# ScalarE's first two DMAs in a top-2 expert combine change places

## Chip, cores and metric

The kernel runs on one core of one Trainium2 chip. The metric is the device time of one execution in microseconds (us), taken as the median of several runs. A program page of the profile describes one execution of it. Engines are named as there: DVE is VectorE, ACT is ScalarE, SP is SyncE (it only issues transfers here), POOL is GpSimd. A name with a q behind it (ACTq, SPq) is the part of an engine that issues DMAs and waits.

## Reference

Each of 16 x 1024 tokens has two expert outputs of 512 numbers and two weights. The result is the weighted sum of the two.

```python
def setup_inputs():
    batch, seq, hidden, n_experts, k = 16, 1024, 512, 8, 2
    # expert_outputs (batch, seq, k, hidden), combine_weights (batch, seq, k), float32
def reference(expert_outputs, combine_weights):
    weights = combine_weights[..., np.newaxis]
    return np.sum(expert_outputs * weights, axis=2).astype(np.float32)
```

So 67 MB are read, 34 MB are written, and there are two multiplications and one addition for each number of the output.

## The kernel before, in words

The 16384 tokens are spread over 128 partitions, 128 tokens to each: the first 115 of a partition's tokens are neighbours in memory, and so are its last 13. A partition's share is worked through in ten tiles of 13, 13, 12, 13, 13, 13, 12, 13, 13 and 13 tokens. SBUF has room for four tiles (the array `et`); tile g lies in room g modulo 4, and the result of a tile overwrites the front half of a room, from where it is stored.

**Tiles 0 to 7** take two DVE instructions each: a multiplication of the whole tile by its weights, in place (L98), and an addition of the two halves (L99). Tile 8 is shared between ACT (L91) and DVE (L93, L95, L99). Tile 9 is done token by token, ACT multiplying one half (L74) and DVE doing the rest (L75).

**Transfers.** SP issues the loads (L68). Tile 0 is loaded in two pieces: two tokens in rows cut to 4 KB (called load 0a here, 256 rows of 4 KB) and the other eleven (load 0b, 128 rows of 45 KB). Loads 1, 2 and 3 follow, 128 rows of 48 or 52 KB each. Load 4 and the later ones each wait until the result that used their room has been stored. The stores of tiles 0 to 6 are issued by ACT (L121), the last two by SP: one for tiles 7 and 8 together, and one for tile 9.

**Around the change.** The order of instructions is written by hand; on each engine they stand in the order of the code. DVE's first instruction (L102) fills a small tile `zt` (16 partitions x 128 numbers) with zeros. ACT's first three instructions are DMAs: `zt` to 16 places of the output, 512 bytes each (L105); the main weights, 230 numbers for each partition, which serve tiles 0 to 8 (L71, called by the first `weights(...)`); and the last tile's weights, 26 numbers for each partition (L71, the second call). The zeros are overwritten later by the store of the results; the first store waits for them. Then comes a small ACT instruction that has the activation table loaded (L108). DVE's first multiplication (L98 of tile 0) waits for load 0a, load 0b and the main weights.

The queue of SP's DMAs is q1 in the profile, that of ACT's is q10. Each DMA over 128 partitions gives each of 16 DMA engines eight data packets (load 0a sixteen) and one packet of 4 bytes that signals the end; the zeros give each engine one data packet and one signal.

Of the kernel before, what the change touches and what calls it, by code (L numbers as in the profile page):

```python
# [1 line left out]

# [4 lines left out]


@with_exitstack
def kernel(  # L10
    ctx: ExitStack,
    tc: tile.TileContext,
    expert_outputs: bass.AP,
    combine_weights: bass.AP,
    out: bass.AP,
):

    nc = tc.nc
    b, s, k, h = expert_outputs.shape
    assert k == 2
    n = b * s
    P = nc.NUM_PARTITIONS
    per = n // P
    assert per * P == n

    SIZES = [13, 13, 12, 13]
    ROOMS = len(SIZES)  # L30
    ROOM0 = [sum(SIZES[:r]) for r in range(ROOMS)]
    TILES = [13, 13, 12, 13, 13, 13, 12, 13, 13, 13]
    FIRST = [2, 11, 13, 12, 13]
    STORES = [[0], [1], [2], [3], [4], [5], [6], [7, 8], [9]]
    MIXED = {8: 3}
    LAST = 115
    N = len(TILES)
    assert sum(TILES) == per
    starts = [sum(TILES[:g]) for g in range(N)]

    def rows(x):

        first = x[0 : P * LAST, :].rearrange("(p t) f -> p t f", p=P)
        second = x[P * LAST : n, :].rearrange("(p t) f -> p t f", p=P)
        return lambda t, c: first[:, t : t + c, :] if t < LAST else second[:, t - LAST : t - LAST + c, :]

    flat = out.rearrange("b s h -> (b s) h")
    eo = rows(expert_outputs.rearrange("b s k h -> (b s) (k h)"))
    cw = rows(combine_weights.rearrange("b s k -> (b s) k"))
    o = rows(flat)  # L50

    dt = mybir.dt.float32
    mult = mybir.AluOpType.mult
    add = mybir.AluOpType.add
    copy = mybir.ActivationFunctionType.Copy

    pool = ctx.enter_context(tc.tile_pool(name="all", bufs=1))
    et = pool.tile([P, sum(SIZES), k * h], dt)
    halves = et.rearrange("p j (k h) -> p (j k) h", k=k)
    wt = pool.tile([P, per * k], dt)  # L60
    wk = wt.rearrange("p (t k) -> p t k", k=k)
    zt = pool.tile([16, 128], dt)
    warm = pool.tile([P, 1], dt)

    def load(g, skip=0, c=None, **kw):
        c = TILES[g] - skip if c is None else c
        at = ROOM0[g % ROOMS] + skip
        nc.sync.dma_start(out=et[:, at : at + c], in_=eo(starts[g] + skip, c), **kw)  # L68

    def weights(q, t, c):  # L70
        q.dma_start(out=wk[:, t : t + c, :], in_=cw(t, c))  # L71

    def pair(t, x0, x1, y):
        nc.scalar.activation(out=x0, in_=x0, func=copy, scale=wt[:, k * t : k * t + 1])  # L74
        nc.vector.scalar_tensor_tensor(  # L75
            out=y, in0=x1, scalar=wt[:, k * t + 1 : k * t + 2], in1=x0, op0=mult, op1=add
        )

    def combine(g, base):
        at, c, t0 = ROOM0[g % ROOMS], TILES[g], starts[g]  # L80
        room = halves[:, k * at : k * (at + c), :]
        x0, x1 = et[:, at : at + c, 0:h], et[:, at : at + c, h : 2 * h]
        if g == N - 1:
            for i in range(c):
                pair(t0 + i, x0[:, i, :], x1[:, i, :], halves[:, base + i, :])
            return
        if g in MIXED:
            v = MIXED[g]
            for i in range(v, c):
                x = x0[:, i, :]  # L90
                nc.scalar.activation(out=x, in_=x, func=copy, scale=wt[:, k * (t0 + i) : k * (t0 + i) + 1])  # L91
            w0 = wk[:, t0 : t0 + v, 0:1].to_broadcast([P, v, h])
            nc.vector.tensor_tensor(out=x0[:, 0:v, :], in0=x0[:, 0:v, :], in1=w0, op=mult)  # L93
            w1 = wk[:, t0 : t0 + c, 1:2].to_broadcast([P, c, h])
            nc.vector.tensor_tensor(out=x1, in0=x1, in1=w1, op=mult)  # L95
        else:
            wb = wt[:, k * t0 : k * (t0 + c)].unsqueeze(2).to_broadcast([P, k * c, h])
            nc.vector.tensor_tensor(out=room, in0=room, in1=wb, op=mult)  # L98
        nc.vector.tensor_tensor(out=halves[:, base : base + c, :], in0=x0, in1=x1, op=add)  # L99

    with tc.manual_schedule():
        nc.vector.memset(zt, 0.0)  # L102

        ahead = flat[0 : P * LAST, :].rearrange("(q t) h -> q (t h)", q=16)
        nc.scalar.dma_start(out=ahead[:, 0:128], in_=zt)  # L105
        weights(nc.scalar, 0, LAST)
        weights(nc.scalar, LAST, per - LAST)
        nc.scalar.activation(out=warm, in_=nc.const_aps.tensor(1.0, (P, 1), dt), func=copy)  # L108

        load(0, 0, 2, max_dma_last_dim=k * h * 4)  # L110
        load(0, 2)
        for g in range(1, ROOMS):
            load(g)
        for j, st in enumerate(STORES):
            base = k * ROOM0[st[0] % ROOMS if st != [N - 1] else (N - 4) % ROOMS]
            c = 0
            for g in st:
                combine(g, base + c)
                c += TILES[g]
            q = nc.sync if j in (7, 8) else nc.scalar  # L120
            q.dma_start(out=o(starts[st[0]], c), in_=halves[:, base : base + c, :])  # L121
            for g in st:
                if g + ROOMS < N:
                    load(g + ROOMS)


# [1 line left out]
_INS = ['expert_outputs', 'combine_weights']  # L128
_OUTS = [((16, 1024, 512), 'float32')]


# [23 lines left out]
```

## Time and profile before

| what | value |
|---|---|
| median of 3 runs | 238.88 us (238.88 to 238.91) |
| the profiled execution's own time | 238.91 us |
| its span, first to last record | 237.1 us |
| DVE busy | 190.0 us |
| ACT busy | 15.8 us |
| HBM traffic | 100.80 MB, 425 GB/s over the span |

The profiled execution is the slowest of the three runs' range, 0.03 us above the median. Its time is 1.8 us longer than its span. The span's start is the zero of all times in the views. A line such as `1.43 18.04 DMA wt<-in_combine_weights_dram` in the chain reads: from 1.43 us on, for 18.04 us, the chain was a transfer into `wt`. A row of the list of issues ends with KB for each and the median time from issue to landing. A row of a DMA queue in a window gives packets, MB, and the packets' time as a share of the 16 engines' time in that window (packets are counted where they start, so that long ones can bring a short window above 100%).

### The profile page before, as it was taken

The numbers are of one execution on the slowest core, as the hardware profiler recorded it, in microseconds if no ns is written. First come the engines' busy times: TensorE is split into PE (matmuls) and PEld (weight loads), VectorE is DVE, ScalarE is ACT, GpSimd is POOL, SyncE is SP. The second block draws the span as 40 slices with busy tenths as digits, with TensorE's granted clock in tenths as the row PEclk, the third lists the DMA queues.
The fourth block names the chain that finished last, engine by engine and source line by source line (L and its number), as shares of the span: only waits on it lengthen the run. The fifth ranks groups of instructions, "written<-read, shape, count | busy, mean of one in ns | idle before, by whom it ended". The sixth has DMA issues, their size and how long they took to land.

```text
span 237.1 us, 153 instructions
## 1 busy us (share of the span) xinstructions
DVE 190.0 (80%) x33; ACT 15.8 (7%) x25; POOL 0.2 (0%) x4
## 2 busy tenths in 40 slices
DVE  0007999999999999999999998998499969919400
ACT  2000000000000000000000000000000055019200
POOL 0000000000000000000000000000000000000000
DMA  8999999989999998999899998999899999899996
GB/s 300 458 411 434 432 421 415 453 375 458 431 449 449 449 440 381 486 420 420 368 483 409 409 517 384 431 503 431 359 431 503 420 397 492 372 431 431 431 431 287
DMA packets 3328, 100.80 MB, mean 425 GB/s; under 512 B 496, under 2 KB 640, under 8 KB 896
## 3 DMA queue, kind: packets, MB, share of 16 engines
q1 hardware_dynamic: 2000, 77.33, 75.9%
q10 hardware_dynamic: 1328, 23.47, 23.0%
HBM read 67.24 MB, written 33.56 MB: 425 GB/s over the span
## 4 chain that ended last, share of the span: by engine, by line
DVE 53%; DMA 36%; issue 3%; ACT 0%; DVEq 0%; ACTq 0%; SPq 0%
DVE et L98 35%; DMA out_dram<-et 17%; DVE et L99 15%; DMA et<-in_expert_outputs_dram 12%; DMA wt<-in_combine_weights_dram 8%; DVE et L75 3%; ACT et L74 0%; DVEq L150 0%; ACTq L105 0%; DVE zt L102 0%; DVEq L98 0%; SPq L68 0%; ACTq L74 0%
## 5 line engine op out<-in xcount | busy, mean ns | idle before, releaser
L98 DVE TENSOR_TENSOR et<-et,wt 128x13312 f32<-128x13312 f32 (+1 forms) x8 | 110.0, 13754 | 23.7 <-DMA wt<-in_combine_weights_dram 18.6
L99 DVE TENSOR_TENSOR et<-et 128x6656 f32<-128x6656 f32 (+1 forms) x9 | 62.8, 6973 | 0.4
L91 ACT ACTIVATE et<-et,wt 128x512 f32<-128x512 f32 x10 | 6.2, 707 | 188.6 <-DMA et<-in_expert_outputs_dram 188.6
L75 DVE SCALAR_TENSOR_TENSOR et<-et,wt 128x512 f32<-128x512 f32 x13 | 8.7, 745 | 5.1 <-ACT et L74 5.1
L74 ACT ACTIVATE et<-et,wt 128x512 f32<-128x512 f32 x13 | 8.1, 707 | 14.0 <-DMA et<-in_expert_outputs_dram 14.0
L95 DVE TENSOR_TENSOR et<-et,wt 128x6656 f32<-128x6656 f32 x1 | 7.1, 7083 | 0.0
L93 DVE TENSOR_TENSOR et<-et,wt 128x1536 f32<-128x1536 f32 x1 | 1.8, 1758 | 2.2 <-DMA et<-in_expert_outputs_dram 2.2
L108 ACT ACT_TABLE_LOAD x1 | 1.3, 1283 | 2.4 <-issue 2.4
L102 DVE MEMSET zt<- 16x128 f32 x1 | 0.2, 165 | 0.8 <-PEq L139 0.8
L108 ACT ACTIVATE warm<-const-float32-1.0 128x1 f32<-128x1 f32 x1 | 0.2, 203 | 0.0
L139 POOL MEMSET const-bfloat16-1.0<- 128x1 bf16 x1 | 0.1, 102 | 0.0
L139 POOL MEMSET const-uint8-127<- 128x1 uint8 x1 | 0.1, 102 | 0.0
L139 POOL MEMSET const-float32-0.0<- 128x1 f32 x1 | 0.1, 99 | 0.2 <-issue 0.2
L139 POOL MEMSET const-float32-1.0<- 128x1 f32 x1 | 0.1, 99 | 0.0
## 6 DMA issues: line engine op xcount, KB each, us to landing
et<-in_expert_outputs_dram SPq DMA_DIRECT2D x7, 6656.0 KB, 32.2
out_dram<-et ACTq DMA_DIRECT2D x5, 3328.0 KB, 34.8
et<-in_expert_outputs_dram SPq DMA_DIRECT2D x2, 6144.0 KB, 41.0
out_dram<-et SPq DMA_DIRECT2D x1, 6656.0 KB, 19.9
out_dram<-et ACTq DMA_DIRECT2D x2, 3072.0 KB, 37.3
et<-in_expert_outputs_dram SPq DMA_DIRECT2D x1, 5632.0 KB, 18.1
out_dram<-et SPq DMA_DIRECT2D x1, 3328.0 KB, 14.0
et<-in_expert_outputs_dram SPq DMA_DIRECT2D x1, 1024.0 KB, 4.8
```

The costliest lines, as they stand in the source:

```text
L74: nc.scalar.activation(out=x0, in_=x0, func=copy, scale=wt[:, k * t : k * t + 1])
L75: nc.vector.scalar_tensor_tensor(out=y, in0=x1, scalar=wt[:, k * t + 1 : k * t + 2], in1=x0, op0=mult, op1=add)
L91: nc.scalar.activation(out=x, in_=x, func=copy, scale=wt[:, k * (t0 + i) : k * (t0 + i) + 1])
L93: nc.vector.tensor_tensor(out=x0[:, 0:v, :], in0=x0[:, 0:v, :], in1=w0, op=mult)
L95: nc.vector.tensor_tensor(out=x1, in0=x1, in1=w1, op=mult)
L98: nc.vector.tensor_tensor(out=room, in0=room, in1=wb, op=mult)
L99: nc.vector.tensor_tensor(out=halves[:, base : base + c, :], in0=x0, in1=x1, op=add)
L102: nc.vector.memset(zt, 0.0)
L108: nc.scalar.activation(out=warm, in_=nc.const_aps.tensor(1.0, (P, 1), dt), func=copy)
L139: nc = _bacc.Bacc("TRN2", target_bir_lowering=False, num_devices=1)
```

## The change

The main weights' DMA is issued first on ACT, and the zeros' DMA second. The last tile's weights stay third. Nothing else in the code changes.

```diff
         nc.vector.memset(zt, 0.0)

         ahead = flat[0 : P * LAST, :].rearrange("(q t) h -> q (t h)", q=16)
+        weights(nc.scalar, 0, LAST)
         nc.scalar.dma_start(out=ahead[:, 0:128], in_=zt)
-        weights(nc.scalar, 0, LAST)
         weights(nc.scalar, LAST, per - LAST)
         nc.scalar.activation(out=warm, in_=nc.const_aps.tensor(1.0, (P, 1), dt), func=copy)
```

In the built program the order of the instructions differs only there. Two numbers of the semaphores that signal the ends of DMAs change places with the DMAs, and load 4 gets one more wait, for the main weights.

## The prediction

> **What bounds the kernel now.** I read the page first: busy times, the slices, the queues.
>
> ```profile
> span 237.1 us, 153 instructions
> DVE 190.0 (80%) x33; ACT 15.8 (7%) x25; POOL 0.2 (0%) x4
> DMA  8999999989999998999899998999899999899996
> q1 hardware_dynamic: 2000, 77.33, 75.9%
> q10 hardware_dynamic: 1328, 23.47, 23.0%
> HBM read 67.24 MB, written 33.56 MB: 425 GB/s over the span
> ```
>
> DVE, the busiest compute engine, works 80% of the span. The DMA engines' row is 8 or 9 in every slice but the last, and the two queues' packets took 75.9 + 23.0 = 98.9% of what sixteen engines have in 237.1 us, that is 234.5 us. So nearly all of the time is one long, full stream of packets. If it has no gap, its end is set by its bytes and by when it starts to run at full rate, and nothing that only makes an engine wait less can move it.
>
> The chain of waits tells another story at first sight:
>
> ```profile
> 1.01 0.39 ACTq L105
> ...
> 1.43 18.04 DMA wt<-in_combine_weights_dram
> 19.47 0.04 DVEq L98
> ...
> 19.55 14.04 DVE et L98
> ...
> 144.44 39.37 DMA out_dram<-et
> ...
> 183.86 28.78 DMA et<-in_expert_outputs_dram
> ...
> 212.72 0.73 ACT et L74
> ```
>
> It begins with ACT issuing the zeros (L105), goes on through the main weights for 18.04 us, and DVE starts at 19.55. Taken by itself this says that earlier weights mean an earlier DVE and an earlier end. Two checks speak against that. First, DVE's first multiplication waits for load 0b as well, so I looked for that one in the list of issues and in the timeline of the first 2 us:
>
> ```profile
> et<-in_expert_outputs_dram SPq DMA_DIRECT2D x1, 5632.0 KB, 18.1
> ...
> et<-in_expert_outputs_dram SPq DMA_DIRECT2D x1, 1024.0 KB, 4.8
> wt<-in_combine_weights_dram ACTq DMA_DIRECT2D x1, 115.0 KB, 18.0
> out_dram<-zt ACTq DMA_DIRECT2D x1, 8.0 KB, 3.8
> ```
>
> ```profile
> 0.73 0.44 SPq L68 DMA_DIRECT2D et<-in_expert_outputs_dram  x1
> 0.81 0.17 DVE L102 MEMSET zt<- 16x128 f32 x1 [0.81 <-PEq L139]
> ```
>
> ```profile
> 1.22 0.46 SPq L68 DMA_DIRECT2D et<-in_expert_outputs_dram  x1
> 1.43 0.45 ACTq L71 DMA_DIRECT2D wt<-in_combine_weights_dram  x1
> ```
>
> Load 0b is issued at 1.22 and lands 18.1 later, at 19.32; the weights land at 1.43 + 18.04 = 19.47. A wait for several things is put down to the last: behind the weights stands load 0b, only 0.15 us earlier. Second, the tail. The chain's last transfer needs room in the stream, not an earlier request:
>
> ```profile
> 208.44 0.35 SPq L121 DMA_DIRECT2D out_dram<-et  x1
> ```
>
> ```profile
> 222.21 0.34 SPq L121 DMA_DIRECT2D out_dram<-et  x1
> ```
>
> ```profile
> out_dram<-et SPq DMA_DIRECT2D x1, 6656.0 KB, 19.9
> ...
> out_dram<-et SPq DMA_DIRECT2D x1, 3328.0 KB, 14.0
> ```
>
> The store of tiles 7 and 8 is issued at 208.44 and lands at 228.3; tile 9's store is issued at 222.21, 6.1 us before that, on the same queue, and lands at 236.2. The engines go from the one to the other with work to spare. DVE could be several us earlier or later and tile 9's store would still find the stream full. So what bounds the kernel is the stream, from its first packet to its last.
>
> **The change, part by part.** What becomes of the first packets is in the queues' rows of short windows: 1.8 to 3, 3.7 to 4.5, 4.6 to 6.3 and 6.3 to 18.2 us.
>
> ```profile
> q1 hardware_dynamic: 65, 0.27, 95.6%
> ...
> DMA packets 65, 0.27 MB, mean 222 GB/s; under 512 B 0, under 2 KB 0, under 8 KB 65
> ```
>
> ```profile
> q1 hardware_dynamic: 80, 0.33, 99.4%
> q10 hardware_dynamic: 32, 0.01, 4.5%
> ```
>
> ```profile
> q1 hardware_dynamic: 65, 0.86, 117.8%
> ```
>
> ```profile
> q1 hardware_dynamic: 112, 5.05, 97.9%
> q10 hardware_dynamic: 112, 0.10, 2.5%
> ...
> DMA packets 224, 5.15 MB, mean 433 GB/s; under 512 B 0, under 2 KB 112, under 8 KB 112
> ```
>
> The zeros' 32 packets (16 of data, 16 signals) run between 3.7 and 4.5 us, among load 0a's 4 KB packets. From 4.6 to 6.3, where load 0b's 45 KB packets begin, q10 has none. From 6.3 to 18.2 it has 112 weight rows beside 112 packets of 45 KB: one row, one long packet, in turn, seven times on each engine. One such pair takes 11.9 us / 7 = 1.70 us. This is why 115 KB take 18.04 us: the weights came too late for the turns beside the 4 KB packets.
>
> *The weights go first.* ACT's first issue waited for DVE's zeros (0.81 + 0.17 = 0.98) and began at 1.01. The weights need no such wait. ACT should be free at about the time of SP (0.73) and DVE (0.81); I take 0.8, an estimate, against 1.43: 0.6 us earlier, and with no zeros ahead. If they then need the zeros' 3.7 - 1.01 = 2.7 us to their first packet, they begin at 3.5, and most of their eight turns fall beside 4 KB packets, of which one engine's takes 0.99 x 0.8 us x 16 / 80 = 0.16 us. They would land between 6 and 10 us. If they need much longer, they gain one turn, 1.7 us, and land near 17.8. Both are before load 0b's 19.32, so DVE's start hangs on load 0b either way.
>
> *Load 0b* has nearly the same bytes ahead of it. New ahead of its last packet: the eighth weight row, 2.5% x 11.9 us x 16 / 112 = 0.04 us, and up to eight rows of the last tile's weights (104 bytes each, surely no dearer than the 920-byte ones: at most 0.34 us, by their bytes about 0.04). So load 0b lands at 19.3 to 19.7, I take 19.4, and DVE starts 0.1 us earlier (19.45), with ends of 0.15 earlier and 0.2 later.
>
> *What DVE's start is worth:* nothing at the end. The work that hides it is the stream itself. Without that cover it would be worth its own 0.1 us.
>
> *The zeros go second.* They issue behind the weights, at about 0.8 + 0.45 = 1.25, and DVE's memset is over by 0.98, so they wait for nothing. Their two packets on an engine come behind eight weight rows. The first store waits for them, the last tile's weights stand behind them, and load 4 now waits for the main weights as well:
>
> ```profile
> 40.74 0.35 ACTq L121 DMA_DIRECT2D out_dram<-et  x1
> ```
>
> ```profile
> 67.75 0.33 SPq L68 DMA_DIRECT2D et<-in_expert_outputs_dram  x1
> ```
>
> Store 0 is issued at 40.74, load 4 at 67.75, and the last weights are used at 212.72: all tens of us later than the worst landing above. Cost 0; if the zeros were 20 us late, still 0.
>
> *The activation table load* behind ACT's third DMA begins after the same three issues, some 0.2 us sooner; ACT's next real work is after 190 us. Cost 0.
>
> *The stream itself.* Bytes and packets are the same, so only gaps count. There is one visible gap: between 1.8 and 3 us the engines moved 222 GB/s, against 433 from 6.3 to 18.2. That is 1.2 x (1 - 222 / 433) = 0.58 us lost. The weights' eight rows cost 8 x 0.04 = 0.34 us wherever they stand in the full stream; if they run in that gap they are free: at best -0.34 us. At worst they push load 0a's or 0b's packets back (below). No row shows weight packets there, so the term has two ends, -0.34 and +1.0; I take 0, since even the 2.7 us of the nearest row puts their first packet at 3.5, behind the gap.
>
> **Sum.** 0 (DVE) + 0 (zeros, table) + 0 (stream) = the profiled execution's 238.91, which is 0.03 above the median 238.88. Forecast: 238.9 us, no change.
>
> **Rivals.**
>
> *Slower: the two queues' packets are made by one maker, in the order of issue.* For it: the first load's packets came 1.8 - 0.73 = 1.1 us after their issue, the zeros' only 2.7 us after theirs, as if something had first to get through load 0a. If so, the maker was at load 0a from 0.73 to 3.7 - 1.1 = 2.6, 1.9 us for 272 packets or 7 ns each. Weights issued at 0.8 then stand ahead of load 0b (1.22), with 144 packets: 1.0 us. It decides once load 0b's packets are ready later than load 0a's are used up; before, load 0b ran as soon as 4.7 us, and how much earlier it was ready can't be seen. With no slack it costs up to 1.0 us: 239.9. Against: load 0a's own packets fill the engines until about 5 us, and the weights' rows fill 0.34 us more.
>
> [...]
>
> *Faster: the early weights fill the gap at 1.8 to 3 us.* Filled by the weights alone it gives -0.34: 238.6, which is within 0.2%. To be faster than that, load 0a must also start up better because the zeros' write no longer falls among its packets; the whole gap is 0.58: 238.3. Against: in the zeros' window q1 held 99.4%, so the zeros held up nothing.
>
> *The change doesn't do what it says:* the weights still start late and keep alternating with 45 KB packets. They still land at 17.8 to 19.5, and the time is 238.9.
>
> *The chain's reading:* DVE starts when the weights land, say at 8 us, and all moves by 11 us. Load 0b's 19.32 excludes it.
>
> **How the numbers follow.** A difference of 0.2%, 0.48 us, is about what a measurement of this kernel can tell from no change. Forecast as worked out, 238.9: 0.62. Weights still late, 238.9: 0.10. Gap filled by the weights, 238.6: 0.08. Gap gone, 238.3: 0.06. One maker, 239.9: 0.14. The first three are within 0.2%: 0.80; faster 0.06; slower 0.14. The range must hold the first three: 238.5 to 239.5, the upper end with half of the maker's price.
>
> **What would show it.** In the changed kernel's profile: weight packets on q10 from about 3.5 us among the 4 KB packets (right) or none before 6 us (the change did not reach them); DVE's first L98 waiting for load 0b instead of the weights and starting at 19.3 to 19.7; the last store landing at 236.2; queue shares summing to the same 234.5 us. A window between 4.6 and 6.3 in which 16 engines are not full would show the slower rival; a rate above 222 GB/s before 3 us the faster one. The forecast is wrong if the stream has more or less idle time than now, wherever that is.

## The result, and the profile after

| | before | after |
|---|---|---|
| median | 238.92 us (14 runs, 238.86 to 239.10) | 239.84 us (14 runs, 239.34 to 241.09) |
| profiled execution | 238.91 us, span 237.1 | 240.59 us, span 238.8 |

The medians differ by 0.92 us, and the ratio of after to before over all runs is 1.0045 (95% interval 1.0030 to 1.0061): slower. The forecast was 238.9, with a range up to 239.5. The scatter is part of the result: before, all runs lie within 0.24 us; after, within 1.75 us, nine of them from 239.3 to 240.1 and five from 240.6 to 241.1. The profiled execution is one of the five.

First the page of the changed kernel, its span and the queues' rows.

```profile
span 238.8 us, 153 instructions
...
q1 hardware_dynamic: 2000, 77.33, 75.4%
q10 hardware_dynamic: 1328, 23.47, 22.9%
HBM read 67.24 MB, written 33.56 MB: 422 GB/s over the span
```

The same packets and bytes took 98.3% of 238.8 us, 234.7 us per engine; before it was 98.9% of 237.1, 234.5 us. **The work of the engines is almost unchanged, yet the end is 1.7 us later.** So there is more idle time somewhere. A window at the very end finds it: from 236.1 us on, first before, then after.

```profile
DMA packets 0, 0.00 MB, mean 0 GB/s; under 512 B 0, under 2 KB 0, under 8 KB 0
```

```profile
DMA packets 5, 0.05 MB, mean 28 GB/s; under 512 B 3, under 2 KB 3, under 8 KB 3
q1 hardware_dynamic: 5, 0.05, 6.6%
```

Before, nothing starts after 236.1. After, three signals of 4 bytes and two data packets of 26 KB start there. All 23 DMAs of either trace end with sixteen signals (23 x 16 = 368 of the page's 496 packets under 512 B; the other 128 are the rows of 104 bytes), by this count one for each engine. So 13 engines had ended, a fourteenth was about to (its signal starts at 236.19 us), and two had a whole packet to go (both signals at 237.59). Two engines finish alone, 1.4 us behind the rest. The trace also keeps the time of each signal, which no view prints: the median of the last store's sixteen comes at 236.09 us before and 236.26 after, but the last one at 236.25 and 237.93.

Where did they fall behind? The first microseconds of the changed kernel, in the timeline and the list of issues:

```profile
0.72 0.44 ACTq L71 DMA_DIRECT2D wt<-in_combine_weights_dram  x1
```

```profile
et<-in_expert_outputs_dram SPq DMA_DIRECT2D x1, 5632.0 KB, 18.6
...
et<-in_expert_outputs_dram SPq DMA_DIRECT2D x1, 1024.0 KB, 5.7
wt<-in_combine_weights_dram ACTq DMA_DIRECT2D x1, 115.0 KB, 4.7
out_dram<-zt ACTq DMA_DIRECT2D x1, 8.0 KB, 8.5
```

The weights are now issued at 0.72, at the same moment as load 0a, and land at 5.4 us instead of 19.47. Load 0a, though, lands 5.7 us after its issue instead of 4.8. A landing here is that of the slowest engine: load 0a's last signal comes at 6.43 us, the median of its sixteen at 5.77. The chain shows DVE starting later, not earlier, since load 0b is now the last:

```profile
1.20 18.60 DMA et<-in_expert_outputs_dram
...
19.93 14.04 DVE et L98
```

The window from 1.8 to 3 us, where before q1 had 65 packets and the rate was 222 GB/s:

```profile
DMA packets 75, 0.23 MB, mean 192 GB/s; under 512 B 0, under 2 KB 24, under 8 KB 75
...
q1 hardware_dynamic: 51, 0.21, 79.8%
q10 hardware_dynamic: 24, 0.02, 7.1%
```

The weights' rows do run in the gap that the faster rival wanted to see filled, but the rate is 192 GB/s: load 0a has 14 packets fewer there, worth 14 x 0.16 = 2.2 us of engine time, and the 24 rows took 7.1% x 1.2 x 16 = 1.4. How much of this the rows caused isn't shown: three runs below that start as the kernel before does (e4_two_engines, f4_half_skew, g3_late_skew) have 53, 70 and 71 packets in this window, at 181, 239 and 242 GB/s. The signals show the lag itself: load 0a's last signal comes 0.66 us behind their median, against 0.25 before.

The lag then grows. Once stores run beside loads, load packets of 52 KB and store packets of 26 KB start in turn, and before the change, from 53 to 80 us, in groups of sixteen: the engines are in step, all load and then all store. From 59.1 to 59.8 us all sixteen start a load packet, and from 61.1 to 61.5 a store packet:

```profile
q1 hardware_dynamic: 16, 0.85, 280.9%
```

```profile
q10 hardware_dynamic: 16, 0.43, 246.8%
```

That is 280.9% x 0.7 x 16 / 16 = 1.97 us for each load packet and 246.8% x 0.4 x 16 / 16 = 0.99 us for each store packet. After, from 60.4 to 60.7, two engines start theirs alone:

```profile
q1 hardware_dynamic: 2, 0.11, 97.2%
```

97.2% x 0.3 x 16 / 2 = 2.33 us for each. These two packets, out of step and partly beside the stores of the other engines (fourteen store packets from 61.18 us on), took 0.36 us longer, and so the late engines became later. But being out of step isn't enough for that. From 78.80 to 78.95 us two engines again start a load packet alone, 1.7 us behind the rest:

```profile
q1 hardware_dynamic: 2, 0.11, 163.8%
```

163.8% x 0.15 x 16 / 2 = 1.97 us, as in step. What lengthens some of the packets before about 75 us and none like these later isn't shown.

How the lag goes on from there is in the signals. The table has, in us, how far the last of a DMA's sixteen signals comes behind their median, in the one profiled execution of each kernel; f1_gate and e3_small_first are described below.

| kernel (time of this execution) | load 0a | load 1 | load 2 | store 0 | load 3 | last store |
|---|---|---|---|---|---|---|
| before (238.91) | 0.25 | 0.25 | 0.17 | 0.16 | 0.18 | 0.16 |
| after (240.59) | 0.66 | 0.64 | 0.97 | 1.47 | 1.70 | 1.67 |
| f1_gate (238.95) | 0.27 | 0.28 | 0.29 | 0.26 | 0.25 | 0.25 |
| e3_small_first (240.94) | 0.57 | 0.59 | 1.28 | 2.03 | 2.23 | 2.21 |

After the change the lag is 0.64 us when load 1 lands (35.6 us). The rest is made between 41 and 78 us, while the first stores run beside loads 2 and 3, and then it stays the same to the end.

### The profile page after: what moved, and what is told of

It is laid out like the page before. It is cut to its first block, busy times and chain, and to the rows that moved or that the text cites. A ratio compares the mean times of both kernels' runs of the same rounds, so it can differ in the third digit from the quotient of the medians.

```text
span 238.8 us, 153 instructions
## 1 busy us (share of the span) xinstructions
DVE 190.1 (80%) x33; ACT 15.8 (7%) x25; POOL 0.2 (0%) x4
## 4 chain that ended last, share of the span: by engine, by line
DMA 63%; DVE 30%; DVEq 0%; ACT 0%; issue 0%; SPq 0%; ACTq 0%
DMA et<-in_expert_outputs_dram 33%; DMA out_dram<-et 29%; DVE et L98 18%; DVE et L99 9%; DVE et L75 3%; ACT et L74 0%; DVEq L150 0%; SPq L68 0%; DVEq L98 0%; ACTq L74 0%
```

## The experiments

Theory A, formed from the traces: a DMA gives each engine a fixed share, nothing evens the engines out, and the last one sets the end; weight rows among load 0a's first packets leave one or two engines behind. The rivals: it is the zeros, that are now written later (B); that the two engines ACT and SP issue their first DMA at one moment (E); or that early weight rows are bad whatever runs beside them (F). The diffs are against the kernel before, those of e2_late and h2_short_gate against the changed one; in them `src` is the input seen in 16 rows, as `ahead` is the output, and `ws` the main weights in 128 rows. The table puts the kernels side by side. "ACT's packets" are q10's packets, signals included, that start from 1.7 to 3.7 us.

| kernel | ACT's first DMA issued | ACT's packets by 3.7 us | median us (lowest to highest) |
|---|---|---|---|
| before | 1.01 | 0 | 238.92 (238.86 to 239.10) |
| after | 0.72 | 73 | 239.84 (239.34 to 241.09) |
| e1_no_zeros | 0.72 | 70 | 239.68 (239.44 to 239.86) |
| e2_late | 0.79 | 68 | 239.62 (238.91 to 239.79) |
| e3_small_first | 0.73 | 144 | 239.48 (239.39 to 241.89) |
| g2_load_waits | 0.73 | 158 | 239.29 (238.88 to 241.23) |
| h2_short_gate | 0.90 | 45 | 238.93 (238.85 to 239.09) |
| g4_sixteen_rows | 0.73 | 32 | 238.89 (238.85 to 238.96) |
| f1_gate | 1.02 | 0 | 238.94 (238.90 to 239.18) |
| g1_gate_no_zeros | 1.02 | 0 | 238.99 (238.90 to 241.05) |
| f3_early_places | 0.72 | 0 | 238.97 (238.88 to 240.99) |
| h1_half_rows | 0.72 | 0 | 238.88 (238.81 to 240.75) |

### Is it the zeros?

**e1_no_zeros**: the changed kernel without the zeros.

```diff
-        nc.scalar.dma_start(out=ahead[:, 0:128], in_=zt)
         weights(nc.scalar, 0, LAST)
```

> The changed kernel without the zeros' DMA; the output is the same, since the zeros are overwritten anyway. Theory A (the weights' rows among the first packets of load 0a leave one or two DMA engines behind, and the last engine sets the end): as slow and as scattered as the changed kernel, 239.3 to 241, with one or two engines' last packets 0.5 to 2 us behind the others. Rival B (it is the place of the zeros: written at 5 to 7 us instead of 4 us, beside the 45 KB packets): without them back to 238.9, last packets within 0.3 us of each other.

239.68, 1.0032 of before (1.0020 to 1.0044). Without zeros it is as slow, so B falls: the place of the zeros isn't the cause. The lag was smaller than foreseen: in its profile only signals start after 236.1, and the last comes 0.77 us behind the median.

**g1_gate_no_zeros**: no zeros, and the weights held back by a fill of eight numbers of their tile on DVE.

```diff
         nc.vector.memset(zt, 0.0)
+        nc.vector.memset(wt[:, 0:8], 0.0)
...
-        nc.scalar.dma_start(out=ahead[:, 0:128], in_=zt)
```

> The main weights first, held back to 1.02 us by a tiny fill of their tile as in f1_gate, and no zeros at all (they are overwritten anyway). Theory A2 (what counts is that ACT's rows are not made ready together with load 0a's; issued 0.3 us after it they run from 3.9 us): 238.9 to 239.0, as f1_gate. Rival B2 (the zeros are needed too, as f2_late_no_zeros could suggest): 239.4 or more. If f2's 240.8 was only DVE's start at 24.9, this one has DVE at 19.4 to 19.6 and 238.9.

238.99, 1.0008 (0.9994 to 1.0022), with one of twelve runs at 241.05. The zeros aren't needed, only something that delays ACT's first DMA.

### Is it the order, or the moment?

**f1_gate**: the changed kernel's order, weights first and zeros second, with that same fill.

```diff
         nc.vector.memset(zt, 0.0)
+        nc.vector.memset(wt[:, 0:8], 0.0)
...
+        weights(nc.scalar, 0, LAST)
         nc.scalar.dma_start(out=ahead[:, 0:128], in_=zt)
-        weights(nc.scalar, 0, LAST)
```

> The changed kernel with one more thing: a tiny fill of the weights' tile by DVE, which the main weights' DMA waits for. It is issued at about 1.1 us instead of 0.72, weights first and zeros second as in the changed kernel. Theory A (the weights' rows fall among load 0a's first packets, at 2.1 to 4.9 us in the changed kernel): the rows still fall there, at about 2.5 to 5, so 239.3 to 241. Rival E (what unsettles the start is that ACT issues its first DMA at the same moment as SP its first): they are 0.3 us apart again as before the change, so 238.9.

238.94, 1.0001 (0.9993 to 1.0010). This run decides most. Its issue, and its queue from 1.8 to 3 us:

```profile
1.02 0.38 ACTq L71 DMA_DIRECT2D wt<-in_combine_weights_dram  x1
```

```profile
DMA packets 75, 0.31 MB, mean 256 GB/s; under 512 B 0, under 2 KB 0, under 8 KB 75
...
q1 hardware_dynamic: 75, 0.31, 98.6%
```

Load 0a has these 1.2 us to itself and moves 256 GB/s. I had expected the rows to fall there all the same; issued 0.3 us later, the first of them ran at 3.9 us instead of 2.1. **The order of the DMAs cost nothing. What the change took away is the 0.3 us by which ACT's first DMA, waiting for the zeros' fill, came behind SP's.**

**h2_short_gate**: as f1_gate, with the small fill ahead of the zeros' fill.

```diff
+        nc.vector.memset(wt[:, 0:8], 0.0)
         nc.vector.memset(zt, 0.0)
```

> As f1_gate, but the tiny fill stands ahead of the zeros' fill, so that the main weights are issued at about 0.9 us, some 0.18 behind SP's first DMA instead of 0.3. If any clear lead of SP's issue is enough for load 0a's rows to be made first: the weights' rows run from about 3.8 us and 238.9. If the making of load 0a begins later than that (SP's issue takes 0.44): rows from 2.3 us and 239.3 or more.

```profile
0.90 0.38 ACTq L71 DMA_DIRECT2D wt<-in_combine_weights_dram  x1
```

```profile
q10 hardware_dynamic: 45, 0.04, 6.5%
```

238.93, 1.0002 (0.9993 to 1.0011). The rows ran from 3.0 us (45 of them by 3.7), and this was harmless. In e1_no_zeros 16 rows ran before 3 us and 54 more by 3.7, and it was slow. So the delicate time seems to be load 0a's first microsecond or so, up to 3 us, when before the change the engines moved 222 GB/s and not yet 433; no run varies that moment alone.

**e2_late**: the table load ahead of ACT's DMAs, meant to delay them.

```diff
+        nc.scalar.activation(out=warm, in_=nc.const_aps.tensor(1.0, (P, 1), dt), func=copy)
         weights(nc.scalar, 0, LAST)
         nc.scalar.dma_start(out=ahead[:, 0:128], in_=zt)
         weights(nc.scalar, LAST, per - LAST)
-        nc.scalar.activation(out=warm, in_=nc.const_aps.tensor(1.0, (P, 1), dt), func=copy)
```

> The changed kernel's order of DMAs, but ACT's table load goes ahead of all three, so that the weights are issued at about 2.2 us instead of 0.72 and their rows come after load 0a's first packets. Theory A: the engines start evenly again; 238.8 to 239.0, as before the change. Rival B (zeros behind the weights are what costs): 239.3 to 241, since the zeros still stand second and land even later.

```profile
0.72 1.28 ACT L105 ACT_TABLE_LOAD   x1 [0.72 <-PEq L139]
...
0.79 0.40 ACTq L71 DMA_DIRECT2D wt<-in_combine_weights_dram  x1
```

The edit didn't do what it was for: the DMA was issued at 0.79, while the table load ran. 239.62, 1.0023 (1.0013 to 1.0033): six of eight runs near 239.6, two at 238.9. As a variant of the changed kernel with 0.07 us of delay it agrees with A, and tells nothing against B.

**f3_early_places**: the places filled from the input, without a wait.

```diff
-        nc.scalar.dma_start(out=ahead[:, 0:128], in_=zt)
+        nc.scalar.dma_start(out=ahead[:, 0:128], in_=src[:, 0:128])
```

> The kernel before, but the 16 places are filled from the input instead of from the zeros' tile, so that their DMA waits for nothing and is issued at 0.72, with SP's first, and the main weights right behind it at about 1.2. (The places are overwritten later.) Theory A, if the first DMA holds the weights' rows back as the zeros did: 238.9; if it doesn't, rows from about 2.6 us and 239.3 or more. Rival E (two first DMAs at one moment): 239.3 to 241 whenever the rows run.

238.97, 1.0008 (0.9994 to 1.0022), one of twelve runs at 240.99. ACT and SP issue at the same moment here, at 0.72 and 0.73, so E in that form falls; none of ACT's packets ran before 3.7 us.

### How many rows, and beside what?

**e3_small_first**: the last tile's weights first, the main weights third.

```diff
+        weights(nc.scalar, LAST, per - LAST)
         nc.scalar.dma_start(out=ahead[:, 0:128], in_=zt)
         weights(nc.scalar, 0, LAST)
-        weights(nc.scalar, LAST, per - LAST)
```

> The last tile's weights first, the zeros second, the main weights third. As in the changed kernel 128 rows are issued at 0.72 beside load 0a, but of 104 bytes instead of 920. Theory A, if the number of early rows counts: 239.3 to 241. Theory A, if their bytes count (8 x 0.04 us on an engine against 8 x 0.01): 238.9 to 239.3. Rival C (only the main weights themselves matter, because DVE needs them): 238.9, as before the change, since they are late again.

```profile
q1 hardware_dynamic: 42, 0.17, 61.2%
q10 hardware_dynamic: 134, 0.01, 11.6%
```

239.48, 1.0033 (1.0016 to 1.0049). From 1.8 to 3 us load 0a had 42 packets, beside 134 of the 104-byte rows and their signals. It isn't the bytes, and not the main weights in particular.

**g4_sixteen_rows** and **h1_half_rows**: the first 16, or 64, partitions' weights, then the zeros, then the other partitions'.

```diff
+        nc.scalar.dma_start(out=wk[0:16, 0:LAST, :], in_=ws[0:16])     # h1: 0:64
         nc.scalar.dma_start(out=ahead[:, 0:128], in_=zt)
-        weights(nc.scalar, 0, LAST)
+        nc.scalar.dma_start(out=wk[16:P, 0:LAST, :], in_=ws[16:P])     # h1: 64:P
```

> The main weights cut in two: 16 partitions' rows first (one for each engine), then the zeros, then the other 112 partitions, then the last tile's weights. One row per engine is made ready together with load 0a instead of eight. Theory A2, if the number of early rows counts: near 238.9 to 239.2. If a single row at that moment is enough: 239.3 or more, as the changed kernel.

238.89, 0.9998 (0.9989 to 1.0007). One early row for each engine did no harm here.

> The main weights cut in two: 64 partitions' rows first at 0.72 (four rows for each engine), then the zeros, then the other 64, then the last tile's weights. Theory A2 by degrees: between g4_sixteen_rows (238.9, one row) and the changed kernel (239.8, eight rows), 239.1 to 239.5. At a threshold below four: 239.4 or more; at a threshold above four: 238.9.

238.88, 1.0006 (0.9993 to 1.0020), one of eleven runs at 240.75. In its profiled execution the rows ran only after 3.7 us although they were issued at 0.72. So it can't tell degrees from a threshold, and that stays open.

**g2_load_waits**: load 0a is held back instead, to 1.03, and the weights keep 0.73.

```diff
         nc.vector.memset(zt, 0.0)
+        nc.vector.memset(et[:, 0, 0:8], 0.0)
...
+        weights(nc.scalar, 0, LAST)
         nc.scalar.dma_start(out=ahead[:, 0:128], in_=zt)
-        weights(nc.scalar, 0, LAST)
```

> The changed kernel turned round: now SP's load 0a is held back to about 1.1 us by a tiny fill of its room, and the main weights keep 0.72. Theory A2 (only making both ready at one moment scatters the engines): the weights run alone and first, the engines start evenly, all of it about 0.3 us later: 239.0 to 239.3, little scatter, two or three tenths between first and last engine at the end. Rival F (weights' rows at 2 to 3 us are bad in themselves, whatever runs beside them): 239.5 or more, scattered.

239.29, 1.0038 (1.0015 to 1.0062), in two groups: seven of twelve runs from 238.9 to 239.5, five from 240.8 to 241.2. My expectation of an even start held for the first group only; the profiled execution (238.94) belongs to it, so the second group wasn't seen. In that execution the weights were issued at 0.73 and landed 2.2 us later, at 2.9, and load 0a's first packet ran at 2.2, so the two still overlapped. Rival F foresaw 239.5 or more, scattered, and got the scatter; the run doesn't refute it, and whether early rows do harm without load 0a beside them stays open.

### Does one engine's lag set the end, and does it grow?

**e4_two_engines** and **f4_half_skew**: the kernel before, with a copy onto two engines behind ACT's third DMA, 26 KB or 13 KB on each. Its places in the output are overwritten later.

```diff
         weights(nc.scalar, LAST, per - LAST)
+        nc.scalar.dma_start(out=ahead[0:2, 128:6784], in_=src[0:2, 0:6656])   # f4: 128:3456, 0:3328
```

> The kernel before, and behind its three first DMAs one more from ACT that copies 2 x 26 KB from the input to two places of the output (overwritten later), so that two DMA engines get about 1 to 2 us of additional work, at about 35 us, and the other fourteen none. Theory A (each engine has a fixed share, nothing evens them out): the end moves by the whole of it, 239.9 to 241, and two engines finish alone; if lag grows where stores begin, by more. Rival D (work is shared out, only the total counts): 2 x 1 us / 16, 239.0.

240.10, 1.0053 (1.0041 to 1.0065). From 36 to 37 us the two additional packets, and from 236.1 us on what is left:

```profile
q10 hardware_dynamic: 2, 0.05, 12.3%
```

```profile
DMA packets 4, 0.05 MB, mean 28 GB/s; under 512 B 2, under 2 KB 2, under 8 KB 2
```

12.3% x 1 us x 16 / 2 = 0.98 us of work on each of two engines of sixteen moved the end by 1.2 us, and two engines finished alone. Rival D's 239.0 is refuted: here the engines shared nothing out.

> As e4_two_engines, with half of the additional bytes on the two engines (2 x 13 KB). There 26 KB moved the median from 238.9 to 240.1, 1.2 us. Theory A with a plain sum (the end is that of the last engine, lag is carried unchanged): +0.3 to +0.6, 239.2 to 239.5. Theory A with growth of lag where stores begin (in the changed kernel's profile two engines went from 0.8 us behind to 1.8): +0.8 or more, 239.7 to 240.5.

```profile
q10 hardware_dynamic: 2, 0.03, 6.2%
```

240.69, 1.0053 (1.0035 to 1.0071): four of ten runs from 239.1 to 239.6, six from 240.7 to 240.9. Over all runs half the work cost as much as the whole (the ratios are the same), but in two groups. The four lost 0.2 to 0.7 us, about what a plain sum of 0.50 us gives; the six lost 1.7 to 2.0, which it can't. In the profiled execution, one of the six, the last signal comes 0.16 us behind the median for load 1, 0.90 for load 2, 1.68 for store 0 and 1.92 for load 3. So lag put in before the stores begin can grow; what decides whether it does wasn't seen.

**g3_late_skew**: the same 13 KB behind the third store, at 81 us.

```diff
             q.dma_start(out=o(starts[st[0]], c), in_=halves[:, base : base + c, :])
+            if j == 2:
+                nc.scalar.dma_start(out=ahead[0:2, 47104:50432], in_=src[0:2, 0:3328])
```

> The kernel before, with the additional 2 x 13 KB of f4_half_skew on two engines issued behind the third store (81 us) instead of at the start. The places are overwritten later. If lag grows only where stores begin (42 to 76 us): it is carried unchanged from here, +0.3 to +0.6, 239.2 to 239.5. If any lag grows at any time: +0.8 to +2, as f4_half_skew (240.7).

239.68, 1.0029 (1.0018 to 1.0040): +0.74 us, in one group (239.5 to 239.8). It is a little above the plain sum's 0.3 to 0.6 and far below f4_half_skew's six slow runs: in these runs the same work did less harm once loads and stores had settled into their turns.

### A late DVE

**f2_late_no_zeros**: no zeros, and the main weights held back by fourteen fills.

```diff
         nc.vector.memset(zt, 0.0)
+        for i in range(14):
+            nc.vector.memset(wt[:, 0 : k * LAST], 0.0)
...
-        nc.scalar.dma_start(out=ahead[:, 0:128], in_=zt)
```

> No zeros (they are overwritten anyway); fourteen fills of the weights' tile by DVE hold the main weights' DMA back to about 3 to 4 us, so that their rows start near 5 us or later, beside the 45 KB packets, as they did before the change. Theory A (only the time of the rows counts): 238.8 to 239.0, last packets within 0.3 us of each other. Rival B2 (the zeros ahead of the weights are needed as well): 239.3 or more.

```profile
6.00 18.77 DMA wt<-in_combine_weights_dram
...
24.89 14.04 DVE et L98
```

```profile
74.00:84.00 10.00, 9.97 (x2) 0.00 (x0) 0.00 (x0) 1.00 1.01 381
```

240.79, 1.0081 (1.0068 to 1.0094). The fills took longer than planned, so the weights were issued at 6.00 and DVE began 5.3 us late; the run can't judge B2, which g1_gate_no_zeros did later. It showed something else: from 74 to 84 us, after SP's queue had waited for room, the rate was 381 GB/s (before the change 426 in that stretch), though the engines' share of busy time was 1.01. In this kernel a start of DVE 5.3 us later wasn't free.

## Why the prediction was wrong

- **The step that failed is "The stream itself. Bytes and packets are the same, so only gaps count", taken at 0.** It treats sixteen engines as one stream with one end. Their work did stay the same (234.5 and 234.7 us), but they ended apart. e4_two_engines showed that 0.98 us of work on each of two engines moved the end by 1.2 us, and f4_half_skew that lag put in early can grow more than threefold (0.50 us of work, 1.7 to 2.0 us lost in six of ten runs). In the changed kernel's profile the last engine is 0.66 us behind at load 0a and 1.67 at the end.
- **The size.** The term had the ends -0.34 and +1.0, and +0.92 was measured. That this lies between them is luck, since the +1.0 was the slower rival's price. The term was taken at 0 because the rows would first run at 3.5 us, and the range took in half of the upper end. The 3.5 came from the zeros' 2.7 us, from a DMA issued 0.3 us after SP's; the weights issued with SP's needed only 1.4.
- **The slower rival had about the right time (239.9) for a wrong reason, by luck.** It put the loss where load 0b comes too late. The window from 4.6 to 6.3 us of the changed kernel has q1 at 144.2%, and with every packet's time cut at the window's ends q1 and q10 still took 102% of the sixteen engines' time; the engines were full. What holds of it is that the order of issue matters: 0.3 us of delay moved the weights' first row from 2.1 to 3.9 us (f1_gate). It isn't all, since in h1_half_rows the first row came at 3.9 us without that delay. One maker for both queues, its 7 ns for a packet and its 1.0 us were my estimates from the zeros' 2.7 us; no run measured them.
- **The faster rival** wanted the gap before 3 us filled. Rows did run there, and the rate was 192 GB/s, not above 222. The difference is within what unchanged starts show (181 to 242).
- **DVE's start** was right in its reason and wrong in its sign. Load 0b did take over from the weights, and the weights' early landing brought nothing, but load 0b landed at 19.80 instead of 19.4, since its slowest engine had been left behind by load 0a (the last signal is 0.66 us behind the median there, and 0.63 at load 0b). "DVE could be several us earlier or later" was too bold: f2_late_no_zeros lost 1.9 us in all with DVE 5.3 us late, though its engines were busy to the end (share 1.00 from 215 to 236 us). A full stream wasn't enough.
- **Zeros, table load, the additional wait: right.** The zeros landed at 9.7 us, far ahead of store 0, and f1_gate with the same order measured no difference.

Still open: why rows among load 0a's first packets leave just one or two engines behind, and whether load 0a has to be beside them (F); what makes the lag grow up to 78 us and stop there; why a lag of 0.37 us at load 0a ended as 0.77 at the last store in e1_no_zeros, and as 0.20 in the profiled execution of g2_load_waits; whether four rows on an engine would do it; and what the second groups near 241 in g2_load_waits, and the single such runs of f3, g1 and h1, look like inside, since none was profiled. Of the changed kernel only one of the five slower runs was profiled; e1_no_zeros and e2_late, at 239.7 like its other nine, end with the last signal 0.77 and 0.68 us behind the median.

## What to carry to other kernels

When DMA engines are busy 99% of the span, don't stop at total bytes: look at the last microseconds, and see whether all sixteen end together. A wait that seems to delay a DMA for nothing may, as here, keep its rows out of another load's start, so before such a wait is removed, see what else is issued in that moment. A short experiment that keeps the new order but restores the old delay separates the two.

## What the runs showed of the hardware that I had not expected

- A load packet of 52 KB took 1.97 us when all engines loaded at once (59.1 to 59.8 us, before). On two engines that loaded partly while the others stored it took 2.33 us at 60.4 us, and again 1.97 at 78.8 (windows above).
- The moment of issue alone didn't settle when ACT's first row ran. Issued at 1.02 us it ran at 3.9 (f1_gate), and at 0.90 at 3.0 (h2_short_gate). Issued at 0.72 or 0.73, with SP's first, it ran at 1.8 (e3_small_first), 2.1 (the changed kernel), 2.5 (g4_sixteen_rows), 2.6 (e1_no_zeros), 3.9 (h1_half_rows) or 4.5 (f3_early_places).
- ACT issued a DMA at 0.79 us while its table load (0.72 to 2.00) still ran (e2_late): there the load didn't hold back the DMA that stands behind it in the code.
